# One encoder layer on one core: the preparations for the last MLP chunks by turns, and the residual added at a chunk's end

## The chip, the core and the metric

The program runs on one core of a Trainium2 chip. The metric is the device time of one execution in microseconds; the figure given for a kernel is the median of its runs.

The engines are TensorE (PE; its weight loads are PEld), VectorE (DVE), ScalarE (ACT), GpSimd (POOL) and SyncE (SP), which issues every DMA here. Each engine works through its own queue in the order of the program, so an instruction that waits holds up all that stands behind it on that engine.

## The reference, cut to what matters

Two request groups, 512 and 1024 tokens of width 1024, go through one layer with shared weights. The time in question lies in the MLP and what directly follows it:

```python
h = h + concat([o_attn, o_pool]) @ w_out
m = rmsnorm(h, norm_mlp_g)
h = h + square(relu(m @ w_up)) @ w_down          # D_FF = 4096
gate = sigmoid(rmsnorm(h, norm_ple_g) @ w_ple_gate)
h = h + gate * (p @ w_ple_proj)                  # then the final rmsnorm
```

All operands are float32.

## The kernel before, in words

**Precision.** TensorE gets fp32r operands. A float32 operand is split into a high part (an ACT cast) and a low part (operand minus high part, on DVE or POOL), and a product is three matmuls: high·high, high·low, low·high.

**Layout.** The 1536 tokens are three chunks (c = 0, 1, 2) of 512 tokens, kept transposed with 128 features on the partitions. Data lives in 49 equal slots of SBUF that tiles take and give back; a new tile waits until the slot's last user, a DMA too, is done.

**The MLP.** It follows the attention stage. A `Pair` (c, g) is two of the 32 blocks of 128 hidden features of one chunk; 16 pairs make a chunk, pair number n runs from 0 to 47. The up product of a pair is done by Strassen-Winograd: seven products `i` in the order `UP = (1, 6, 2, 5, 7, 3, 4)`, each 12 matmuls of 128x256, with operands `w` (weights) and `mo` (inputs, stored by `make_m`). DVE takes the sums out of PSUM (tiles `u`, `c`). Product 3 goes on top of the PSUM bank of product 5 and product 4 on top of that of product 7, so TensorE can start them only after DVE has read those banks (the additions into `u` and into `c[:, B]` after products 5 and 7).

In chunk 0 the down product is plain. In chunks 1 and 2 two pairs together form a `Double`, whose down product is also Winograd: seven products in the order `DOWN = (1, 5, 2, 3, 7, 6, 4)`, 24 matmuls each (tile `pd`), with weights `v` and inputs `ta`. Up and down products alternate on TensorE: the fourteen up products of a double are steps k = 0 to 13, and after each odd k one down product of the double before is issued.

Two streams prepare the operands, one piece at each `next`:

- `weights()` loads four quarters `we` of w_down, forms their sums on DVE (tiles `vs`, `we`) and splits each into `v`: per half an ACT cast and a POOL subtraction.
- `inputs()` splits the activations `c` into `ta`: an ACT cast, a DVE subtraction, and DVE differences.

Both are called once after every step (`after(i)`), so a `v` takes two steps and a `ta` with its difference takes two steps. The streams of a double begin at its own k = 10 and 11, so that two `v` and two `ta` lie ready ahead of its first down product.

**The residual.** mean(h²)+eps is a row `w` of one value per token. The MLP is computed on unnormalised h, so the result has to be divided by `w`. Before, the accumulators start as h·w (`raise_h` for chunk 0; `load_quarters` and `raise_to` for chunks 1 and 2, which store the accumulators as five tiles `H..`: 22, 11, 12, 21 and u), every down product is added to them on DVE, `invert` replaces `w` by its reciprocal, and in the end the accumulator is multiplied by it (`finishing`, `finishing_from`, `stat_h`).

**Chores.** Work that is not urgent is a queue of generators, `chores`; `step()` runs one piece of the first of them after each product. In chunk 1 these are `finishing(0)` and `make_m(2)`, in chunk 2 `finishing_from(1)`.

**DMA.** The split up-weights of pairs 1 to 15 are kept in DRAM by chunk 0 (`kept_d`) and fetched again by chunks 1 and 2: seven loads of 512 KB for each pair, some pieces ahead.

## Time and profile before

| | |
|---|---|
| median of 3 runs | 1802.34 us (1800.7 to 1809.57) |
| profiled execution | 1805.42 us, its span 1803.5 us |
| mean granted TensorE clock | 0.991 |
| PE / DVE / ACT / POOL busy | 96% / 75% / 50% / 59% of the span |
| DMA | 390.73 MB, 217 GB/s on average |
| chunk 0 of the MLP | about 580 to 917 us |
| chunks 1 and 2 | about 917 to 1580 us |
| gate stage and end | from about 1580 us |

A busy PE is not yet a PE at its peak, because matmuls are pipelined. In chunks 1 and 2 all matmuls have one form, 128x256, so their number in a stretch of equal length is the better measure: 338 or 339 in 40 us where nothing is in the way. The prediction counts them.

### The profile page before, as it was taken

The page shows a single profiled execution, that of the slowest core. Times are in us where ns is not written, and L with a number is a line of the kernel's source. Part 1 is how long each engine was busy: PE and PEld are TensorE (multiplying, and loading weights), DVE is VectorE, ACT ScalarE, POOL GpSimd, SP SyncE. Part 2 cuts the span into 40 slices and gives each one's busy share as a digit, 9 for nine tenths or more (in the row PEclk, how much of TensorE's full clock was granted, in tenths as well). Part 3 has the DMA queues.
Part 4 walks back from the last instruction along what each step waited for, and adds up shares of the span by engine and source line. Part 5 has one row for each costly group of instructions (what it writes and reads, how often), then busy time and mean ns, then how long its engine had stood idle before and what let it go on. Part 6 is the DMA issues. An engine that isn't in the chain of part 4 may idle for free. (4 is left out here: it accounts for less than half of the span.)

```text
span 1803.5 us, 31527 instructions
## 1 busy us (share of the span) xinstructions
PE 1736.2 (96%) x11692; PEld 1577.2 (87%) x11692; DVE 1356.7 (75%) x1880; ACT 910.3 (50%) x1830; POOL 1055.1 (59%) x907
## 2 busy tenths in 40 slices
PE   9999999999999899999998999999999999999997
PEld 6888777888868788988998999999999999987797
DVE  5667765888895876876548887889988877876755
ACT  6343455768794455655435454545444444433232
POOL 3474873535675757775626668867577555652421
PEclk9999999999999999999999999999999999999998
DMA  6232645120418899897799877799767777643102
GB/s 249 100 125 105 221 163 191 43 95 13 175 66 329 317 307 340 317 343 270 279 388 328 299 245 255 267 314 362 269 234 273 242 256 238 232 150 111 59 9 86
DMA packets 133608, 390.73 MB, mean 217 GB/s; under 512 B 14160, under 2 KB 26832, under 8 KB 133456
## 3 DMA queue, kind: packets, MB, share of 16 engines
q1 hardware_dynamic: 133456, 388.73, 60.7%
q8 instruction: 92, 1.51, 0.3%
q14 instruction: 60, 0.49, 0.1%
HBM read 274.38 MB, written 114.29 MB: 216 GB/s over the span
## 5 line engine op out<-in xcount | busy, mean ns | idle before, releaser
L49 PE MATMUL pd<-ta,v 128*128 128x256 f32 x2688 | 341.9, 283 | 4.1 <-DVE ta L1023 3.7
L49 PEld LDWEIGHTS pd<-ta,v 128*128 128x128 f32 x2688 | 331.2, 191 | 5.7 <-DVE ta L1023 4.6
L1008 POOL TENSOR_TENSOR v<-we,v 128x512 fp32r<-128x512 f32 x128 | 198.3, 1559 | 88.6 <-ACT v L1007 79.7
L1008 POOL TENSOR_TENSOR v<-vs,v 128x512 fp32r<-128x512 f32 x96 | 141.7, 1480 | 148.9 <-ACT v L1007 137.9
L1023 DVE TENSOR_TENSOR ta<-c,ta 128x512 fp32r<-128x512 f32 x112 | 143.3, 1280 | 73.6 <-ACT ta L1022 70.6
L49 PE MATMUL pd<-r,wd 128*128 128x512 f32 x768 | 191.2, 396 | 4.6 <-DVE r L916 4.1
L461 POOL TENSOR_SCALAR pr<-pr,rr 128x512 f32<-128x512 f32 x160 | 111.5, 708 | 134.1 <-DVE rr L456 64.4
L49 PE MATMUL z<-w,x 128*128 128x512 f32 (+1 forms) x864 | 175.8, 359 | 1.9 <-ACT w L159 1.4
L49 PE MATMUL pq<-mo,w 128*128 128x256 f32 x1152 | 157.0, 287 | 16.7 <-DVE c L951 14.7
L49 PEld LDWEIGHTS pd<-r,wd 128*128 128x128 f32 x768 | 139.6, 188 | 35.8 <-DVE r L916 6.4
L49 PEld LDWEIGHTS z<-w,x 128*128 128x128 f32 x864 | 143.2, 189 | 28.8 <-ACT w L159 3.5
L49 PEld LDWEIGHTS pq<-mo,w 128*128 128x128 f32 x1152 | 146.7, 193 | 18.6 <-DVE c L951 16.1
L49 PE MATMUL pz<-mo,w 128*128 128x256 f32 x1152 | 153.4, 282 | 3.5 <-DVE u L946 3.2
L49 PE MATMUL px<-mo,w 128*128 128x256 f32 x1152 | 152.8, 282 | 1.3 <-DMA w<-kept_d 1.3
L49 PEld LDWEIGHTS pz<-mo,w 128*128 128x128 f32 x1152 | 145.2, 189 | 8.8 <-DVE u L946 5.4
L815 POOL TENSOR_TENSOR w<-ws,w 128x512 fp32r<-128x512 f32 x72 | 102.2, 1423 | 79.9 <-ACT w L814 66.4
L49 PEld LDWEIGHTS px<-mo,w 128*128 128x128 f32 x1152 | 144.7, 189 | 3.2 <-issue 1.4
L49 PE MATMUL pg<-hg,wg 128*128 128x512 f32 (+1 forms) x768 | 142.0, 340 | 0.0
L49 PEld LDWEIGHTS pg<-hg,wg 128*128 128x128 f32 x768 | 119.8, 190 | 17.0 <-DVE s L1525 0.3
L472 ACT CAST pt<-tp 128x512 fp32r<-128x512 f32 x160 | 88.0, 591 | 88.5 <-PE tp L53 86.7
L473 DVE TENSOR_TENSOR pt<-tp,pt 128x512 fp32r<-128x512 f32 x160 | 104.1, 684 | 31.3 <-ACT pt L472 31.0
L441 DVE TENSOR_REDUCE nm<-S 128x1 f32<-128x1024 f32 (+1 forms) x96 | 100.0, 1042 | 23.3 <-PE S L49 22.7
(234 smaller groups left out, 3573.5 us busy)
## 6 DMA issues: line engine op xcount, KB each, us to landing
w<-kept_d SPq DMA_DIRECT2D x210, 512.0 KB, 5.1
kept_d<-w SPq DMA_DIRECT2D x105, 512.0 KB, 5.0
we<-in_w_down_dram SPq DMA_DIRECT2D x64, 512.0 KB, 5.4
mo_d<-mm SPq DMA_DIRECT2D x84, 256.0 KB, 4.8
mo<-mo_d SPq DMA_DIRECT2D x42, 512.0 KB, 8.7
wur<-in_w_up_dram SPq DMA_DIRECT2D x36, 512.0 KB, 5.9
wdr<-in_w_down_dram SPq DMA_DIRECT2D x32, 512.0 KB, 7.2
h_d<-h SPq DMA_DIRECT2D x16, 512.0 KB, 2.9
```

What stands on the lines that cost most here:

```text
L49: last_pe[0] = nc.tensor.matmul(*a, **k).ins
L441: ve.tensor_reduce(nm, S[:, :nch * CH], axis=AX.X, op=ALU.max, negate=True)
L461: gp.tensor_scalar(p, p, rr, 1.0, op0=ALU.mult, op1=ALU.mult)
L472: sc.copy(self.pt[kt][:, 0], tp)
L473: ve.tensor_tensor(self.pt[kt][:, 1], tp, as32(self.pt[kt][:, 0]), op=ALU.subtract)
L815: gp.tensor_tensor(t[:, 1], x, as32(t[:, 0]), op=ALU.subtract)
L1008: gp.tensor_tensor(t[:, 1], src[:, p], as32(t[:, 0]), op=ALU.subtract)
L1023: ve.tensor_tensor(t[:, 1], x, as32(t[:, 0]), op=ALU.subtract)
```

## The change

- **Accumulators.** The first down product of a chunk that goes to an accumulator is copied to it by ACT; `raise_h`, `load_quarters` and `raise_to` are gone, and with them the loads of h at each chunk's start. The residual comes back when a chunk is finished: `finishing(0)` and `lower_from` (chunk 1) multiply by 1/w and then add h, reloaded as `rest`, on POOL. For chunk 2 a new chore `raise_late` multiplies the reloaded h by w on DVE and adds it on POOL, after `finishing_from(1)`.
- **Reciprocals.** They move from `invert` into `make_m`.
- **Turns.** At odd k both streams are called twice, at even k not at all. An ACT cast and a sum take a whole `v` (128x1024) in one instruction; the low part stays two POOL instructions of 128x512, and the first of them waits for the newest DVE instruction of `inputs()`. The streams of a double begin at k = 11, and the loads `we` come up to one step earlier.
- **Layout of `v`.** High and low parts are two tiles of their own instead of halves of two tiles.

```diff
+    wr_d = dram.tile([P, CH], F32, name="wr_d")
...
         ve.tensor_scalar(acc[:, 1], bc, 1.0 / D, EPS, op0=ALU.mult, op1=ALU.add)
+        if c == 2:
+            sy.dma_start(wr_d, acc[:, 1])
+        for b in range(4):
+            yield
+            w = acc[:, 1, b * P:(b + 1) * P]
+            ve.reciprocal(w, w)
         sy.dma_start(w_d[c], acc[:, 1])
...
-    def raise_h(c, e=ve):
-        for a in range(4):
-            for h in range(2):
-                e.tensor_tensor(hT[c][a][:, h], hT[c][a][:, h], ws[c], op=ALU.mult)
-                yield
...
-    def load_quarters(c):
-        HS[c] = {nm: slot([P, D], F32, f"H{c}{nm}") for nm in ("22", "11", "12", "21")}
-        for (q, x), t in HS[c].items():
-            for a in range(2):
-                load(quarters(t[:, a * CH:(a + 1) * CH]), h_d[c][2 * (int(q) - 1) + a][:, :, TOK[x]])
-        HS[c]["u"] = slot([P, D], F32, f"H{c}u")
...
-    def raise_to(c):
-        for nm in ("22", "11", "12", "21"):
-            for a in range(2):
-                scaled(c, nm, a)
-                yield
...
     def lower_from(c, nm, e):
         H = HS[c]
+        r = rest(c, nm) if c < 2 else None
         for a in range(2):
+            part = slice(a * CH, (a + 1) * CH)
+            t = H[nm][:, part]
             if nm != "11":
-                t = H[nm][:, a * CH:(a + 1) * CH]
-                e.tensor_tensor(t, t, H["u"][:, a * CH:(a + 1) * CH], op=ALU.add)
+                e.tensor_tensor(t, t, H["u"][:, part], op=ALU.add)
                 yield
             scaled(c, nm, a)
             yield
+            if r is not None:
+                e.tensor_tensor(t, t, r[:, part], op=ALU.add)
+                yield
+    def rest(c, nm):
+        r = slot([P, D], F32, f"rest{c}{nm}")
+        for a in range(2):
+            load(quarters(r[:, a * CH:(a + 1) * CH]), h_d[c][2 * (int(nm[0]) - 1) + a][:, :, TOK[nm[1]]])
+        return r
+    def raise_late(c):
+        w = slot([P, CH], F32, f"wr{c}")
+        load(w, wr_d)
+        for nm in ("22", "11", "12", "21"):
+            r = rest(c, nm)
+            yield from wait(4)
+            for a in range(2):
+                part = slice(a * CH, (a + 1) * CH)
+                t = quarters(r[:, part])
+                ve.tensor_tensor(t, t, w[:, TOK[nm[1]]].unsqueeze(1).to_broadcast([P, 2, HF]), op=ALU.mult)
+                yield
+                gp.tensor_tensor(HS[c][nm][:, part], HS[c][nm][:, part], r[:, part], op=ALU.add)
+                yield
...
-    def invert(c):
-        for b in range(4):
-            w = ws[c][:, b * P:(b + 1) * P]
-            ve.reciprocal(w, w)
-            yield
-        sy.dma_start(w_d[c], ws[c])
...
-            h = hT[self.c][a]
-            ve.tensor_tensor(h, pd.rearrange("p (a b) -> p a b", a=2), h, op=ALU.add)
+            pd = pd.rearrange("p (a b) -> p a b", a=2)
+            if self.g == 0:
+                h = hT.setdefault(0, {})[a] = slot([P, 2, CH], F32, f"h0{a}m")
+                sc.copy(h, pd)
+            else:
+                h = hT[0][a]
+                ve.tensor_tensor(h, pd, h, op=ALU.add)
...
-            def total(i, p):
-                e = SUMS[i]
-                if i == 1:
-                    e.tensor_tensor(s[0][:, p], e21[:, p], e22[:, p], op=ALU.add)
-                elif i == 2:
-                    e.tensor_tensor(s[1][:, p], s[0][:, p], e11[:, p], op=ALU.subtract)
-                elif i == 4:
-                    e.tensor_tensor(s[0][:, p], e12[:, p], s[1][:, p], op=ALU.subtract)
-                else:
-                    e.tensor_tensor(e21[:, p], e11[:, p], e21[:, p], op=ALU.subtract)
-            at = 0
             for i in DOWN:
                 if i == 5:
                     s.append(slot([P, 2, CH], F32, f"vs{self.id}1"))
+                total = {1: (s[0], e21, e22, ALU.add), 5: (s[-1], s[0], e11, ALU.subtract),
+                         2: (s[0], e12, s[-1], ALU.subtract), 3: (e21, e11, e21, ALU.subtract)}
                 src = {1: e11, 5: s[0], 2: e12, 3: s[0], 7: e21, 6: s[-1], 4: e22}[i]
-                self.v[i] = []
+                hi, lo = self.v[i] = [slot([P, 2, CH], F32R, f"v{self.id}_{i}{k}") for k in range(2)]
+                sc.copy(hi, src)
+                if i in total and i != 2:
+                    out, x, y, op = total[i]
+                    ve.tensor_tensor(out, x, y, op=op)
+                yield
                 for p in range(2):
-                    t = slot([P, 2, CH], F32R, f"v{self.id}_{i}{p}")
-                    self.v[i].append(t)
-                    sc.copy(t[:, 0], src[:, p])
-                    gp.tensor_tensor(t[:, 1], src[:, p], as32(t[:, 0]), op=ALU.subtract)
-                    for what in AT.get(at, ()):
-                        total(*what)
-                    at += 1
-                    yield
+                    ins = gp.tensor_tensor(lo[:, p], src[:, p], as32(hi[:, p]), op=ALU.subtract).ins
+                    if p == 0 and last_ve[0] is not None:
+                        tc.add_manual_dep(ins, last_ve[0].name, SYNC, reason="port")
+                if i == 2:
+                    out, x, y, op = total[i]
+                    ve.tensor_tensor(out, x, y, op=op)
+                yield
...
-            diffs = {1: (b11, b12, b11), 3: (b12, b22, b12), 7: (b11, b22, b11), 6: (b21, b21, b11)}
+            diffs = {3: (b12, b22, b12), 7: (b11, b22, b11), 6: (b21, b21, b11)}
             for i, x in ((1, b11), (5, b11), (2, b21), (3, b22), (7, b12), (6, b11), (4, b21)):
+                if i == 5:
+                    ve.tensor_tensor(b11, b12, b11, op=ALU.subtract)
                 t = self.t7[i] = slot([P, 2, 2, HF], F32R, f"ta{self.id}_{i}")
                 sc.copy(t[:, 0], x)
-                ve.tensor_tensor(t[:, 1], x, as32(t[:, 0]), op=ALU.subtract)
                 yield
+                last_ve[0] = ve.tensor_tensor(t[:, 1], x, as32(t[:, 0]), op=ALU.subtract).ins
                 if i in diffs:
                     out, y, z = diffs[i]
-                    ve.tensor_tensor(out, y, z, op=ALU.subtract)
+                    last_ve[0] = ve.tensor_tensor(out, y, z, op=ALU.subtract).ins
                 yield
...
-                    ws_ = [w[p][:, k, j * P:(j + 1) * P] for k in range(2)]
+                    ws_ = [w[k][:, p, j * P:(j + 1) * P] for k in range(2)]
...
-                h = HS[self.c][{1: "u", 6: "u", 2: "11", 5: "22", 7: "22", 3: "12", 4: "21"}[i]]
-                if i == 1 and self.m == 0:
-                    sc.copy(h, pd)
+                to = {1: "u", 6: "u", 2: "11", 5: "22", 7: "22", 3: "12", 4: "21"}[i]
+                H = HS.setdefault(self.c, {})
+                if to not in H:
+                    H[to] = slot([P, D], F32, f"H{self.c}{to}")
+                    sc.copy(H[to], pd)
                 else:
+                    h = H[to]
                     ve.tensor_tensor(h, pd, h, op=ALU.add)
...
-    SUMS = {1: ve, 2: ve, 3: ve, 4: ve}
-    AT = {0: ((1, 0),), 1: ((1, 1),), 2: ((2, 0),), 3: ((2, 1),), 4: ((4, 0),), 5: ((4, 1),), 6: ((3, 0),), 7: ((3, 1),)}
...
-    LEADS, STEPS = (4, 3), (1, 1)
+    STEPS, last_ve = (1, 1), [None]
+    SYNC = mybir.DependencyInfo(mybir.DependencyClass.Sync, mybir.DependencyReason.DATA)
...
-    LOADS = {3: (0, 0), 6: (0, 1), 8: (1, 1), 10: (1, 0)}
+    LOADS = {3: (0, 0), 5: (0, 1), 7: (1, 1), 9: (1, 0)}
...
+            r = slot([P, 2, CH], F32, f"rest{c}{a}")
+            load(r, h_d[c][a])
             for e in range(2):
                 ve.tensor_tensor(h[:, e], h[:, e], ws[c], op=ALU.mult)
+                yield
+                gp.tensor_tensor(h[:, e], h[:, e], r[:, e], op=ALU.add)
                 yield
...
-        if c == 0 and g == 0:
-            load_ms(c)
-            late_h = raise_h(c)
-        if g == 1:
-            if c:
-                load_ms(c)
-                load_quarters(c)
-                raising = raise_to(c)
-            else:
-                chores.append(invert(c))
...
-        if g == 3 and c:
-            chores.append(invert(c))
...
+            chores.append(raise_late(2))
...
-            if n == 0:
-                load_h(0, i, h_d[0][i])
-            if n == 1:
-                next(late_h)
-                next(late_h)
...
-            if raising and UP.index(i) % 2:
-                next(raising, None)
...
-                if last_db or k >= 14 - LEADS[0]:
+                feed_w, feed_x = k % 2 and (last_db or k >= 11), k % 2 and (last_db or k >= 11)
+                if feed_x:
+                    next(inputs)
+                if feed_w:
                     next(weights)
-                if last_db or k >= 15 - LEADS[1]:
+                if feed_x:
                     next(inputs)
+                if feed_w:
+                    next(weights)
...
-        for _ in range(2):
-            next(weights, None)
-            next(inputs, None)
+        for stream in (inputs, weights, inputs, weights):
+            next(stream, None)
```

Three places show what moves. The first is DVE's queue in the second pair of chunk 2 (`u2_1`, `c2_..` are that pair's tiles, the `vs2_0.` sums of the next double's weights, `H222` an accumulator); before:

```order
L946 TENSOR_TENSOR u2_1_14566<-pz2_1_14682,u2_1_14566 128x256
L658 TENSOR_TENSOR H222_14553<-H222_14553,w2_14551 128x512
L990 TENSOR_TENSOR vs2_00_14702<-we2_001_14543,we2_011_14629 128x512
L1023 TENSOR_TENSOR ta1_7_4_14707<-c1_71_13773,ta1_7_4_14707 128x512
L951 TENSOR_TENSOR c2_01_14314<-pq2_1_14710,u2_1_14566 128x256
```

The same place now:

```order
L1029 TENSOR_TENSOR ta1_7_4_14538<-c1_71_13685,ta1_7_4_14538 128x512
L1060 TENSOR_TENSOR H122_10731<-pd1_77_14546,H122_10731 128x1024
L956 TENSOR_TENSOR u2_1_14451<-pz2_1_14571,u2_1_14451 128x256
L961 TENSOR_TENSOR c2_01_14224<-pq2_1_14588,u2_1_14451 128x256
L1006 TENSOR_TENSOR vs2_00_14606<-we2_001_14398,we2_011_14468 128x1024
L1029 TENSOR_TENSOR ta2_0_1_14604<-c2_00_14223,ta2_0_1_14604 128x512
```

Three SBUF instructions stood between the two readings of PSUM (`u` and `c`, products 5 and 7); now none does, and the sum, twice as wide, stands behind them.

The second is SP's queue early in chunk 1, about the second pair; before:

```order
L56 DMA we1_001_10403<-in_w_down_dram 128x2x512
L56 DMA w1_10419<-w_d1_260 128x512
L56 DMA H122_10421<-h_d1_2_310 128x2x256
L56 DMA H122_10421<-h_d1_3_311 128x2x256
L56 DMA H111_10422<-h_d1_0_308 128x2x256
L56 DMA H111_10422<-h_d1_1_309 128x2x256
L56 DMA H112_10423<-h_d1_0_308 128x2x256
L56 DMA H112_10423<-h_d1_1_309 128x2x256
L56 DMA H121_10424<-h_d1_2_310 128x2x256
L56 DMA H121_10424<-h_d1_3_311 128x2x256
L56 DMA w0_10434<-w_d0_259 128x512
L56 DMA w1_1_7_10451<-kept_d1_7_320 128x1024
```

Now (`rest00` is the residual for `finishing(0)`):

```order
L56 DMA w1_1_5_10393<-kept_d1_5_320 128x1024
L56 DMA w0_10409<-w_d0_260 128x512
L56 DMA w1_1_7_10426<-kept_d1_7_321 128x1024
L56 DMA we1_011_10428<-in_w_down_dram 128x2x512
L56 DMA rest00_10431<-h_d0_0_305 128x1024
L56 DMA w1_1_3_10448<-kept_d1_3_322 128x1024
```

Eight loads ahead of the up-weights `w1_1_7` are gone; one of 512 KB comes in behind it.

The third is POOL's queue at the start of the first double of chunk 1; before:

```order
L1008 TENSOR_TENSOR v1_0_20_10618<-we1_010_10514,v1_0_20_10618 128x512
L1008 TENSOR_TENSOR v1_0_21_10649<-we1_010_10514,v1_0_21_10649 128x512
L1352 TENSOR_TENSOR sqg0_10453<-sqg0_10453,sqg01_10626 128x512
L1008 TENSOR_TENSOR v1_0_30_10696<-vs1_00_10516,v1_0_30_10696 128x512
L1352 TENSOR_TENSOR sqg0_10453<-sqg0_10453,sqg01_10626 128x512
L1008 TENSOR_TENSOR v1_0_31_10723<-vs1_00_10516,v1_0_31_10723 128x512
```

Now:

```order
L1009 TENSOR_TENSOR v1_0_21_10613<-we1_010_10467,v1_0_20_10612 128x512 x2
L1354 TENSOR_TENSOR h01m_6915<-h01m_6915,rest01_10591 128x512
L1009 TENSOR_TENSOR v1_0_31_10685<-vs1_00_10505,v1_0_30_10684 128x512 x2
L1354 TENSOR_TENSOR h01m_6915<-h01m_6915,rest01_10591 128x512
L1009 TENSOR_TENSOR v1_0_71_10765<-we1_001_10376,v1_0_70_10764 128x512 x2
```

The low parts of a `v` now come in twos, and additions of the reloaded residual, each waiting for a DMA, stand between them.

More of the change, by code (lines that the diff above doesn't have):

```diff
@@ L1399, in encoder_layer @@
     START, MORE = 1, (2, 2)
-    before, pending, raising = None, deque(), None
+    before, pending = None, deque()
     for n, pair in enumerate(pairs):
         c, g = pair.c, pair.g
-        if c == 0 and g == 0:
-            load_ms(c)
-            late_h = raise_h(c)
-        if g == 1:
-            if c:
-                load_ms(c)
-                load_quarters(c)
-                raising = raise_to(c)
-            else:
-                chores.append(invert(c))
         if (c, g) == (1, 1):
@@ L1483, in encoder_layer @@
             pass
-        if g == 3:
-            for _ in raising or ():
-                pass
-            raising = None
         before = pair
```

## The prediction

> **What bounds the kernel now.** I read the head of the page first: who is busy.
>
> ```profile
> span 1803.5 us, 31527 instructions
> PE 1736.2 (96%) x11692; PEld 1577.2 (87%) x11692; DVE 1356.7 (75%) x1880; ACT 910.3 (50%) x1830; POOL 1055.1 (59%) x907
> ```
>
> TensorE is the bound: whatever the other engines save counts only where TensorE stands still or runs slowly for their sake. So the next view is the table of stretches over chunks 1 and 2 (start:end, length, PE busy and number of matmuls, then PEld, DVE, ACT, POOL, granted clock, DMA share, GB/s).
>
> ```profile
> 960.00:1000.00 40.00, 33.59 (x260) 32.37 (x259) 36.40 (x40) 17.78 (x34) 25.23 (x16) 0.93 0.85 309
> 1080.00:1120.00 40.00, 39.27 (x329) 39.03 (x328) 30.46 (x32) 20.78 (x41) 34.14 (x24) 1.00 0.69 230
> 1120.00:1160.00 40.00, 37.08 (x301) 36.88 (x300) 32.02 (x34) 21.07 (x41) 29.55 (x21) 0.96 0.86 314
> 1160.00:1200.00 40.00, 38.45 (x321) 38.04 (x320) 33.21 (x35) 21.18 (x42) 34.79 (x24) 1.00 0.88 288
> 1320.00:1360.00 40.00, 36.97 (x295) 36.36 (x295) 36.82 (x41) 17.58 (x32) 28.73 (x21) 0.96 0.73 253
> 1360.00:1400.00 40.00, 38.40 (x324) 38.19 (x323) 35.37 (x38) 16.71 (x33) 28.94 (x22) 1.00 0.69 249
> 1440.00:1480.00 40.00, 40.00 (x339) 40.00 (x338) 30.62 (x37) 17.32 (x35) 21.74 (x15) 1.00 0.72 238
> ```
>
> The last row is the undisturbed state: 339 matmuls of 128x256 in 40 us, 0.118 us each. Against it 79 are missing from 960 to 1000 (9.3 us), 10 + 38 + 18 = 66 from 1080 to 1200 (7.8 us), 44 + 15 = 59 from 1320 to 1400 (7.0 us): 24 us in all. This count holds both the idle time and the slow matmuls behind it, for the granted clock is 0.93 and 0.96 in three of these rows and 1.00 in the undisturbed one. These 24 us, and little else, are what a better order of the preparations can win.
>
> The waits of TensorE between 955 and 1560 us say for whom (total, times, longest):
>
> ```profile
> PE pq L49 <- DVE c L951: 12.8, 5, 4.1
> PE pz L49 <- DVE u L946: 3.2, 7, 1.0
> ```
>
> Both are DVE reading a PSUM bank on which TensorE wants to accumulate the next up product. DVE's own timeline shows why it is late, ahead of the longest of them and of the one in chunk 2:
>
> ```profile
> 990.77 1.56 DVE L658 TENSOR_TENSOR H<-H,w 128x512 f32<-128x512 f32 x1
> 992.25 1.75 DVE L990 TENSOR_TENSOR vs<-we,we 128x512 f32<-128x512 f32 x1
> 993.92 1.74 DVE L1023 TENSOR_TENSOR ta<-c,ta 128x512 fp32r<-128x512 f32 x1
> 995.59 0.74 DVE L1327 SCALAR_TENSOR_TENSOR hg<-h,gple_sb,hg 128x512 fp32r<-128x512 f32 x1
> 996.26 0.41 DVE L951 TENSOR_TENSOR c<-pq,u 128x256 f32<-128x256 f32 x1
> ...
> 1328.69 1.58 DVE L658 TENSOR_TENSOR H<-H,w 128x512 f32<-128x512 f32 x1
> 1330.19 1.75 DVE L990 TENSOR_TENSOR vs<-we,we 128x512 f32<-128x512 f32 x1
> 1331.86 0.68 DVE L1023 TENSOR_TENSOR ta<-c,ta 128x512 fp32r<-128x512 f32 x1
> 1332.46 0.41 DVE L951 TENSOR_TENSOR c<-pq,u 128x256 f32<-128x256 f32 x1
> ```
>
> Preparations (raising the accumulator, a weight sum, an input's low part) stand in the queue ahead of the urgent reading, and most of them take 1.6 to 1.75 us.
>
> **The change part by part.** Prices first (minimum/median/maximum in ns):
>
> ```profile
> L658 DVE TENSOR_TENSOR H<-H,w x32: 674/693/1786, 943.8 to 1708.9; 128x512 f32<-128x512 f32 x32
> L1052 DVE TENSOR_TENSOR H<-pd,H x80: 1154/1211/1226, 971.0 to 1653.8; 128x1024 f32<-128x1024 f32 x80
> L1050 ACT COPY H1u<-pd x1: 1008/1008/1008, 961.9 to 961.9; 128x1024 f32<-128x1024 f32 x1
> L1023 DVE TENSOR_TENSOR ta<-c,ta x112: 672/1365/1861, 953.9 to 1635.5; 128x512 fp32r<-128x512 f32 x112
> L1008 POOL TENSOR_TENSOR v<-we,v x128: 1262/1730/1826, 948.1 to 1628.3; 128x512 fp32r<-128x512 f32 x128
> ```
>
> A DVE instruction with two SBUF operands has two prices, 0.67 and about 1.75, and so has POOL's, 1.26 and 1.73; the one that reads PSUM has a single price, 1.15 to 1.23. So DVE and POOL slow each other down in SBUF, and the urgent readings of PSUM suffer only from what stands ahead of them.
>
> *Start of chunk 1, loads.* The eight loads of H sit in SP's queue ahead of the up-weights, and TensorE then waits for those weights:
>
> ```profile
> 927.69 9.03 SPq L56 DMA_DIRECT2D H<-h_d  x8
> 937.73 1.06 SPq L56 DMA_DIRECT2D w<-kept_d  x2
> 951.49 1.67 PE L49 MATMUL px<-mo,w 128*128 128x256 f32 x12 [1.26 <-DMA w<-kept_d]
> 954.49 1.70 PE L49 MATMUL py<-mo,w 128*128 128x256 f32 x12 [1.33 <-DMA w<-kept_d]
> ```
>
> The 9.0 us of issuing become one load of 512 KB. The two waits, 2.6 us, can at most vanish; the weights come up to 9 us earlier, so I take 2.5.
>
> *Start of chunk 1, DVE (960 to 1000).* DVE loses the eight raisings of chunk 1 (0.67 to 1.56 us each here, so between 5.4 and 12.5 us) and four first additions, 4 x 1.21 = 4.8 us, which become copies on ACT at 1.01 us, an engine that is busy for 17.8 of the 40 us. That is 10 to 17 us off an engine that was busy for 36.4 of 40 and late by 4.1 at the worst place. Bounds: 0 and 9.3; I take 7.5, near the upper end, since the relief is more than twice the longest lateness, less a part for the first two `v`, which now begin a step later.
>
> *Chunk 1, 1080 to 1200.* There is nothing to raise here. The worst wait is one for a slot:
>
> ```profile
> 1122.31 1.45 DVE L990 TENSOR_TENSOR vs<-we,we 128x512 f32<-128x512 f32 x1 [3.76 <-DMA mo_d<-mm]
> 1124.76 2.93 PE L49 MATMUL pq<-mo,w 128*128 128x256 f32 x12 [2.92 <-DVE c L951]
> ```
>
> The sum needed a slot that a store had not yet freed, and the reading of `pq` stood behind it. In the new order no sum stands between the two readings in the second pair of a double; the sum comes after, where the next urgent reading has a down product (24 x 0.118 = 2.8 us) and two up products (1.4 each) before TensorE needs it; these 5.7 us I call a round. In the first pair the feeding at k = 3 does stand between them, but with a down product in between: product 7, down and product 3 give the same 5.7 us or more. The feeding then is a sum of 128x1024 (two of 128x512: 1.35 to 3.5 us) and two of 128x512 (1.35 to 3.5): 2.7 us if POOL is quiet, 7.0 if it is not. So slot waits of up to 3 us are hidden when POOL is quiet and partly show when it is not. Bounds 0 and 7.8; I take 5.
>
> *Chunk 2, 1320 to 1400.* The raisings go (they become `raise_late`, a chore in the later, undisturbed part), and the order is the new one. Bounds 0 and 7.0; I take 5.
>
> *Chunk 0.* The eight raisings and the four loads of its first pairs go, and ACT makes four copies. The longest wait of TensorE among the second pair's down products, where the raisings run, is this:
>
> ```profile
> 620.94 2.13 PE L49 MATMUL pd<-r,wd 128*128 128x512 f32 x8 [0.89 <-DVE r L916]
> ```
>
> Its releaser belongs to the chain of the activation, not to the raising; bounds 0 and 0.9, and I count nothing.
>
> *The rest of chunk 2 and the gate stage.* Undisturbed rows stay so; the gate stage keeps its instructions. Nothing. The reciprocals only change their place, as chores of DVE: nothing, as long as DVE is not late there.
>
> Sum of the gains: 2.5 + 7.5 + 5 + 5 = 20 us.
>
> *What is added.* POOL gets 8 additions for each chunk, 24 x 1.26 to 1.73 = 30 to 42 us. Their cover is POOL's own waiting (in the stretch from 940 to 1600 us):
>
> ```profile
> POOL v L1008 <- ACT v L1007: 208.6, 80, 21.1
> ```
>
> With 208.6 us of it I cost them at nothing; without that cover they cost up to 42. The waits that come with them are another matter. `finishing(0)` loads each of its four `rest` one step before POOL wants it, and `lower_from` does so for the part "11"; a like load takes 5.9 us to land:
>
> ```profile
> m<-h_d SPq DMA_DIRECT2D x12, 512.0 KB, 5.9
> ```
>
> A step is 2.9 us with its share of the down products, so POOL may stand for 3 us, five times, and behind it the next `v`. A `v` is begun two rounds ahead, 2 x 5.7 = 11.4 us; its sum, its two partners on DVE and its two POOL halves take 2.7 + 2.5 = 5.2 us without contention and 7.0 + 3.5 = 10.5 with it. So the standing is hidden or shows in part: 0 to 15 us, and I take 2, since both cases have to coincide. The new wait of POOL for DVE holds up the chores behind it, and DVE in turn waits for POOL before a sum may overwrite a source (product 2's) and at each multiplication in `lower_from`. The trace of before has no such ring; its bounds are nothing and, for 16 doubles with one such sum each of up to 1.7 us late, 27. I take 0, for the readings behind it have 5.7 us.
>
> Net: 20 - 2 = 18 us. Made against the profiled execution (1805.42 us, span 1803.5) that is 1787; this execution was 3.1 us above the median of the runs, 1802.34, so the forecast for the median is 1784 us.
>
> A rule speaks against the turns. The Trainium skill, "SBUF — State Buffer", section "SBUF: two separate sides", says that the port pair shared by VectorE and GpSimd is an exclusive lock held for the whole instruction and not a division of the bandwidth. The two prices above agree in that there is a quick and a slow one. They don't in full: 0.67 us of DVE inside 1.26 us of POOL would make 1.93 for the one that waits and 1.26 for the other, and the rows have 1.73 to 1.78 for both. By that rule turns win nothing in total, and the first rival below is what it would do here.
>
> **The rivals.** *Slower: POOL becomes the bound in the parts with chores.* From 1160 to 1200 POOL is already busy for 34.8 of 40 us. In a round of 5.7 us it has two halves of a `v` and two chores, 4 x 1.26 = 5.0 us if DVE keeps off and 4 x 1.73 = 6.9 if not, and now it waits for DVE as well. It decides as soon as a round takes longer than 5.7 us for so many rounds that the 11.4 us ahead are used up; then the added 30 to 42 us reach TensorE and the gains are lost in part: 30 - 20 = 10 to 42 - 20 = 22 us slower, about 1816. Against it: a stretch of chores in which every piece has POOL work is short, the long ones were survived before at the same load, and 208.6 us of waiting are free.
>
> *No change that counts: the lateness only moves.* The wide sum (1.35 to 3.5 us) and the slot waits stay, now in front of other readings. Then only the loads (2.5 us) and half of 960 to 1000 (4.6) are won, less 2: about 1797. For it speaks that the worst wait from 1080 to 1200 is a DMA's.
>
> *All of it.* 2.5 + 9.3 + 7.8 + 7.0 = 27 us: about 1775.
>
> **How the numbers follow.** I give the forecast 0.53, all of it 0.13, the mere move 0.21, the slower case 0.13. A measurement of this kernel can tell about 0.5%, 9 us, from no change: faster is under 1793, slower over 1811. Faster gets 0.53 + 0.13 = 0.66, the same 0.21, slower 0.13. The range reaches from 1768 (all of it, and some of the waits outside the three stretches) to 1804, which takes in the mere move with the full 7 us of its uncertainty; the slower case stays outside.
>
> **What would show it.** In the profile after, 960 to 1000 should have over 320 matmuls and 1320 to 1360 over 330; TensorE's waits for the reading of `pq` (now L961) should fall from 12.8 us to under 4; the `w<-kept_d` waits at the start of chunk 1 should be gone; and these two means should fall, the first towards 0.9 us and the second towards 1.35:
>
> ```profile
> L1023 DVE TENSOR_TENSOR ta<-c,ta 128x512 fp32r<-128x512 f32 x112 | 143.3, 1280 | 73.6 <-ACT ta L1022 70.6
> L1008 POOL TENSOR_TENSOR v<-we,v 128x512 fp32r<-128x512 f32 x128 | 198.3, 1559 | 88.6 <-ACT v L1007 79.7
> ```
>
> POOL should show some 3 us of waiting for each `rest`. I am wrong if TensorE waits for `pd` with POOL's `v` as the releaser, or if the undisturbed rows of 339 fall.

## The result and the profile after

| | median | runs | ratio to before, 95% interval |
|---|---|---|---|
| before | 1803.8 us | 7, 1800.7 to 1809.57 | |
| changed | 1792.95 us | 7, 1791.55 to 1798.7 | 0.9939, 0.9922 to 0.9957 |

The change makes the kernel about 11 us faster. The forecast was 1784 (18 us faster), its range 1768 to 1804. The profiled execution of the changed kernel took 1798.7 us (span 1796.9, mean granted clock 0.990). It is the longest of the seven, so its rows show a little more trouble than the median has.

The head of the page:

```profile
span 1796.9 us, 31417 instructions
PE 1735.9 (97%) x11692; PEld 1579.1 (88%) x11692; DVE 1261.6 (70%) x1788; ACT 908.7 (51%) x1730; POOL 1063.9 (59%) x931
```

VectorE lost 95 us of work, and the time moved by 11. Where the rest went is seen in the stretches over chunks 1 and 2 (same columns as in the prediction):

```profile
920.00:960.00 40.00, 40.00 (x305) 38.47 (x305) 25.34 (x30) 17.95 (x30) 15.35 (x11) 1.00 1.02 384
960.00:1000.00 40.00, 36.72 (x294) 36.31 (x294) 27.06 (x31) 22.13 (x35) 28.76 (x20) 0.96 0.76 285
1000.00:1040.00 40.00, 37.84 (x304) 37.53 (x304) 30.57 (x35) 16.44 (x27) 25.09 (x17) 0.96 0.81 289
1040.00:1080.00 40.00, 37.95 (x306) 37.52 (x305) 26.09 (x34) 16.12 (x28) 22.32 (x18) 0.96 0.77 275
1080.00:1120.00 40.00, 40.00 (x338) 40.00 (x338) 26.37 (x33) 22.90 (x40) 29.50 (x23) 1.00 0.62 211
1120.00:1160.00 40.00, 39.78 (x334) 39.57 (x334) 29.95 (x31) 19.80 (x35) 29.63 (x22) 1.00 0.96 346
1160.00:1200.00 40.00, 38.89 (x325) 38.48 (x324) 30.61 (x32) 22.82 (x39) 34.66 (x24) 1.00 0.73 249
1200.00:1240.00 40.00, 37.81 (x315) 37.31 (x313) 30.53 (x35) 18.51 (x33) 27.15 (x20) 1.00 0.98 369
1240.00:1280.00 40.00, 38.57 (x318) 37.90 (x319) 32.75 (x36) 18.48 (x32) 29.86 (x20) 1.00 0.87 327
1320.00:1360.00 40.00, 37.34 (x312) 36.94 (x311) 28.92 (x32) 14.82 (x24) 32.00 (x24) 1.00 0.65 229
1360.00:1400.00 40.00, 36.85 (x293) 36.23 (x292) 27.53 (x31) 18.20 (x30) 28.82 (x22) 0.96 0.75 264
```

The rows of before that the prediction doesn't show:

```profile
920.00:960.00 40.00, 35.98 (x257) 33.41 (x256) 21.95 (x32) 14.16 (x27) 9.94 (x8) 1.00 1.04 382
1000.00:1040.00 40.00, 40.00 (x333) 40.00 (x332) 31.35 (x38) 19.19 (x37) 26.58 (x19) 0.98 0.85 293
1040.00:1080.00 40.00, 39.90 (x333) 39.61 (x333) 34.86 (x39) 22.68 (x44) 26.47 (x19) 1.00 0.75 244
1200.00:1240.00 40.00, 39.69 (x332) 39.40 (x331) 33.75 (x43) 18.17 (x37) 22.01 (x15) 1.00 0.87 332
1240.00:1280.00 40.00, 39.75 (x334) 39.55 (x334) 36.65 (x40) 20.55 (x41) 32.28 (x21) 1.00 0.91 326
```

Won, in matmuls against before: 305 for 257 from 920 to 960, 294 for 260 from 960 to 1000, 334 for 301 from 1120 to 1160. Lost: 304 and 306 for 333 and 333 from 1000 to 1080, 315 and 318 for 332 and 334 from 1200 to 1280, and 293 for 324 from 1360 to 1400. The first and the last loss are where `finishing(0)` and `finishing_from(1)` run; the one between them is around the start of chunk 2, and the experiments will show that it has another origin. TensorE's waits from 920 to 1600 us name a new releaser, ScalarE:

```profile
PE px L49 <- ACT u L941: 9.4, 8, 2.9
PE pz L49 <- DVE u L956: 4.9, 3, 2.2
PE pq L49 <- DVE c L961: 2.9, 4, 2.0
PE pd L49 <- POOL v L1009: 1.9, 2, 1.1
```

The longest of the new waits, followed back through three queues. TensorE, ScalarE and GpSimd around 966 us:

```profile
973.50 2.00 PE L49 MATMUL px<-mo,w 128*128 128x256 f32 x12 [2.94 <-ACT u L941]
```

```profile
966.59 1.06 ACT L1358 ACTIVATE sqg<-h01m 128x1024 f32<-128x1024 f32 x1 [7.80 <-POOL h01m L1354]
967.55 1.32 ACT L1332 ACTIVATE hg<-h01m,gple_sb 128x512 fp32r<-128x512 f32 x2
...
970.99 1.00 ACT L1057 COPY H<-pd 128x1024 f32<-128x1024 f32 x1
...
973.10 0.35 ACT L941 COPY u<-px 128x256 f32<-128x256 f32 x1
```

```profile
962.77 2.54 POOL L1009 TENSOR_TENSOR v<-vs,v 128x512 fp32r<-128x512 f32 x2 [1.38 <-DVE c L1032]
965.26 1.29 POOL L1354 TENSOR_TENSOR h01m<-h01m,rest 128x512 f32<-128x512 f32 x1
```

Read from below. GpSimd's second residual addition (L1354) stands behind the two halves of a `v`, which wait by the new order for VectorE. ScalarE's square of the sum (L1358) waits for that addition for 7.8 us, and with it the whole queue: two scalings for the gate, a relu and a square of `c`, the casts of `ta` and `v`, the new first copy of `H`, another relu and square. Only then comes the copy of `px` (L941), for which TensorE has been standing. The same happens at 1022 us, where ScalarE waits 5.25 us for `h03m`. There the late cast of `ta` keeps VectorE waiting 6.21 us, and behind that stands the reading of `pz` (a stall of 2.15 us at 1028.14).

In chunk 2 it is VectorE that waits, in `lower_from`, for GpSimd's addition of `u`: 12.7 us in six times.

A stall costs more than its length. In stretches of 10 us around these two the granted clock (third column from the end) falls:

```profile
960.00:970.00 10.00, 10.00 (x86) 10.00 (x86) 3.20 (x5) 3.38 (x6) 5.18 (x4) 1.00 0.58 209
970.00:980.00 10.00, 7.06 (x47) 6.86 (x46) 7.63 (x9) 8.06 (x14) 8.28 (x6) 0.83 0.98 370
...
1020.00:1030.00 10.00, 7.84 (x64) 7.64 (x63) 3.97 (x5) 5.89 (x9) 5.43 (x5) 0.96 0.68 217
1030.00:1040.00 10.00, 10.00 (x76) 10.00 (x76) 9.86 (x11) 3.59 (x7) 6.30 (x4) 0.87 0.72 263
```

From 1030 to 1040 TensorE is never idle and still makes 76 matmuls for the 86 of an undisturbed row. From 960 to 1080 there are 904 matmuls for 3 x 339 = 1017: 113 x 0.118 = 13.3 us lost, with 7.5 us of idle time over 0.3 us each.

### The profile page after: what moved, and what is told of

It is laid out like the page before. It is cut to its first block, busy times and chain, and to the rows that moved or that the text cites. A ratio compares the mean times of both kernels' runs of the same rounds, so it can differ in the third digit from the quotient of the medians.

```text
span 1796.9 us, 31417 instructions
## 1 busy us (share of the span) xinstructions
PE 1735.9 (97%) x11692; PEld 1579.1 (88%) x11692; DVE 1261.6 (70%) x1788; ACT 908.7 (51%) x1730; POOL 1063.9 (59%) x931
## 5 line engine op out<-in xcount | busy, mean ns | idle before, releaser
L1009 POOL TENSOR_TENSOR v<-we,v 128x512 fp32r<-128x512 f32 x128 | 185.0, 1467 | 103.4 <-DVE ta L1029 26.0
L1009 POOL TENSOR_TENSOR v<-vs,v 128x512 fp32r<-128x512 f32 x96 | 128.7, 1363 | 111.5 <-DVE c L1032 37.2
L1029 DVE TENSOR_TENSOR ta<-c,ta 128x512 fp32r<-128x512 f32 x112 | 108.1, 965 | 88.4 <-ACT ta L1027 82.1
```

Source lines behind the costliest of these rows:

```text
L1009: ins = gp.tensor_tensor(lo[:, p], src[:, p], as32(hi[:, p]), op=ALU.subtract).ins
L1029: last_ve[0] = ve.tensor_tensor(t[:, 1], x, as32(t[:, 0]), op=ALU.subtract).ins
```

## The experiments

The theory after this: the additions of the residual cost little as work, but each is a hop to another engine between two instructions of engines whose queues carry urgent readings. Rivals: the work itself costs, wherever it is done; GpSimd is overloaded; the turns' own wide sums make the stalls; only the accumulators bring the gain. Of each kernel 4 to 12 runs were compared with runs of the kernel before on the same chip.

| kernel | median us | ratio to before, 95% interval |
|---|---|---|
| copies_only / copies_added | 1815.12 / 1812.07 | 1.0057 (1.0043 to 1.007) / 1.0044 (1.0029 to 1.0059) |
| turns_only / turns_raised | 1789.69 / 1791.17 | 0.9912 (0.9896 to 0.9928) / 0.9923 (0.9905 to 0.9941) |
| norest | 1774.16 | 0.9831 (0.9811 to 0.9852) |
| sq_later | 1789.36 | 0.9906 (0.9885 to 0.9927) |
| lower | 1790.71 | 0.9914 (0.9897 to 0.9931) |
| add_dve | 1783.47 | 0.9877 (0.9859 to 0.9894) |
| untangled | 1782.17 | 0.988 (0.9858 to 0.9901) |
| dve_later | 1781.08 | 0.9861 (0.9841 to 0.988) |
| mixed_noport | 1788.12 | 0.99 (0.9881 to 0.9919) |
| **mixed** | **1776.32** | **0.9834 (0.9817 to 0.9851)** |

### Either half alone

The streams `weights()` and `inputs()`, their calls, the layout of `v` and the `LOADS` come from one kernel, all the rest from the other. The lines that tell them apart, as taken over or left:

```diff
-                if last_db or k >= 14 - LEADS[0]:
-                    next(weights)
-                if last_db or k >= 15 - LEADS[1]:
-                    next(inputs)
+                feed_w, feed_x = k % 2 and (last_db or k >= 11), k % 2 and (last_db or k >= 11)
+                if feed_x:
+                    next(inputs)
+                if feed_w:
+                    next(weights)
...
+                    if p == 0 and last_ve[0] is not None:
+                        tc.add_manual_dep(ins, last_ve[0].name, SYNC, reason="port")
```

> Only the accumulators: first products copied, residual added at a chunk's end, reciprocals moved; both preparation streams, their calls at every step and the layout of v as before. Theory (queue blocking: the new GpSimd additions sit between a VectorE and a ScalarE instruction and so hold up urgent copies): the wins at the start of chunk 1 appear, the losses from 1000 to 1080 too, the stall near 1122 stays: about 1799 us, 4 less than before. Rival A (the gain is the accumulators' alone, the turns do nothing): 1793, as the changed kernel. Rival B (the accumulators cost more than they bring): 1804 or more.

> Only the turns: both streams twice at odd k, whole-tile casts and sums, the wait of v for the newest VectorE instruction, the new layout; accumulators raised and loaded as before. Theory: 1080 to 1160 gains its 5 us as in the changed kernel, 960 to 1000 stays as bad as before, no new stalls behind the copy of px: about 1798. Rival A (turns do nothing): 1803. Rival C (the wide sums and the wait of v themselves make the new stalls): 1805 or more, with stalls for px and pz as in the changed kernel.

In this first pair a few lines of chunk 0's down product were exchanged too: copies_only adds chunk 0's first products to a tile with stale contents, and turns_only copies them and so lacks chunk 0's residual. The second pair has these lines in their place:

> The turns alone on the kernel before, with its accumulators in all three chunks (turns_only also had chunk 0's copies, and so lacked chunk 0's residual; chunk 0 took 2.6 us less there). Theory 1 (the turns bring the gain, the accumulators cost): 1790 to 1793. Rival A (the turns_only time came from what it lacked): 1800 or more.

> The accumulators alone as in copies_only, but with chunk 0's first products copied too, which copies_only had left as additions to an accumulator with stale contents. Theory 1 (with the preparations in the old order the later additions make VectorE and ScalarE late just as in the changed kernel): 1810 to 1817, slower than before. Rival A (the 1815 came from that slip): 1805 or less.

The turns alone make 1791.17 us, by the ratio some 14 less than before: theory 1 holds, rival A falls. In the first pair I had expected 1798 and no gain from 960 to 1000, and both were wrong: turns_only takes 1789.69 and has 313 matmuls there for 260 before (turns_raised 309). The turns have a loss of their own too: turns_raised has 276 matmuls for 321 from 1160 to 1200, with stalls of 1.93 us for the reading of `pz` and 3.30 us for that of `pq`; the changed kernel has 325 there. The accumulators alone are 7 to 10 us slower than before, as rival B of copies_only had it. I had expected 4 faster in the first pair, and this was wrong; the stale tile was not the reason. In copies_added TensorE waits four times as long for the reading of `pz` as before (3.2 us), and about as long for that of `pq`:

```profile
PE pz L49 <- DVE u L956: 12.4, 10, 3.8
PE pq L49 <- DVE c L961: 11.7, 6, 4.3
```

The longest, 4.34 us at 1206.73, has a sum in front that waits 3.59 us for a load of `we`; in another, at 1401.57, a multiplication of `lower_from` and two slowed preparations stand there. How much of the 7 to 10 us goes to each I have not separated. By place, the largest loss is from 1200 to 1280, around the start of chunk 2: 268 + 309 = 577 matmuls for 666 before, 89 x 0.118 = 10.5 us. The changed kernel has 633 there and turns_raised 678, so this loss comes with the new accumulators, the moved reciprocals included. So the turns account for the whole gain, and the accumulators, as they are written, for none of it.

### Without the additions

```diff
-                gp.tensor_tensor(h[:, e], h[:, e], r[:, e], op=ALU.add)
...
-                e.tensor_tensor(t, t, r[:, part], op=ALU.add)
```

> The changed kernel without the 16 GpSimd additions of the residual in chunks 0 and 1 (finishing(0) and lower_from leave them out, the loads of rest stay; the output lacks that residual; chunk 2 keeps its eight). Theory (queue blocking by these additions): the waits of TensorE for the copy of px fall from 9.4 to under 5 us, the rows from 1000 to 1080 rise from 305 to over 325 matmuls, 1360 to 1400 from 293 to over 320: about 1783 us, 10 less than the changed kernel. Rival C (the turns' own wide sums): within 3 us of the changed kernel's 1793.

1774.16 us, 19 less than the changed kernel; the theory had said 10, rival C at most 3. TensorE's waits for the copy of `px` fall to 3.1 us, and where the finishing chores run the rows are whole:

```profile
960.00:1000.00 40.00, 40.00 (x338) 40.00 (x338) 30.83 (x37) 24.09 (x38) 28.65 (x19) 1.00 0.92 350
1000.00:1040.00 40.00, 40.00 (x339) 40.00 (x338) 32.31 (x40) 19.51 (x32) 25.05 (x17) 1.00 0.91 327
...
1320.00:1360.00 40.00, 40.00 (x339) 40.00 (x338) 28.36 (x35) 18.43 (x31) 27.29 (x22) 1.00 0.83 286
1360.00:1400.00 40.00, 40.00 (x339) 40.00 (x338) 28.08 (x37) 16.89 (x28) 24.85 (x22) 1.00 0.70 261
```

These 16 additions, some 16 x 1.3 to 2.3 us of GpSimd's time, cost 19 us of the kernel's. The loss from 1200 to 1280 is not theirs: without them there are 312 + 319 = 631 matmuls, as in the changed kernel. This alone doesn't tell work from hop; the next four do.

### The hop or the work

The later square: the store, square and first gate input of part a come after the additions of part a + 1.

```diff
-            sy.dma_start(hl_d[c][a], h)
-            sq = slot([P, 2, CH], F32, f"sqg{c}{a}") if a else acc
-            sc.activation(sq, h, AF.Square)
...
+            if a:
+                yield from tail(a - 1)
+        yield from wait(2)
+        yield from tail(3)
```

> The changed kernel with one edit: in finishing(0) the square, the first gate input and the store of a part come after the next part's additions, with the same additions. Theory (ScalarE's square stands waiting for GpSimd's addition, and the copy of px behind it): ScalarE's waits of 7.8 and 5.3 us ahead of the square vanish, and with them the stalls of TensorE at 973 and 1028 (2.9 and 2.2 us) and the slow matmuls behind: 960 to 1080 gains 30 matmuls or more, about 1788. Rival D (GpSimd is overloaded there, whatever waits for it): the stalls move to pd behind v, 1792 or more.

```profile
960.00:1000.00 40.00, 40.00 (x339) 40.00 (x338) 34.04 (x38) 22.69 (x36) 31.79 (x20) 1.00 0.91 346
1000.00:1040.00 40.00, 40.00 (x337) 39.95 (x337) 34.47 (x40) 20.44 (x33) 30.08 (x22) 1.00 0.92 331
1040.00:1080.00 40.00, 40.00 (x337) 39.91 (x336) 24.87 (x35) 18.96 (x32) 20.38 (x18) 1.00 0.69 238
```

From 960 to 1080 there are 339 + 337 + 337 = 1013 matmuls for 904 (theory: at least 30 more), and the stalls at 973 and 1028 are gone, with GpSimd doing the same additions: rival D falls for this place. A part comes back as a loss: from 1120 to 1240 this kernel and the three later ones with the later square have 947 to 952 matmuls, where the changed kernel has 974 and norest 975, some 3 us; why is not shown. The median, 1789.36, is 3.6 us lower, but the two intervals overlap, and its profiled execution (1781.4) is the quickest of its six; the time alone would not have shown it.

The order in `lower_from` (before, the three operations of a half followed each other; `add` is GpSimd's addition of one half):

```diff
...
+        for a in range(2) if nm != "11" else ():
+            add(a, H["u"])
+            yield
+        for a in range(2):
+            scaled(c, nm, a)
+            yield
+        for a in range(2):
+            add(a, r)
+            yield
```

> The changed kernel with one edit: in lower_from the two additions of u, the two multiplications and the two residual additions of a part are issued in that order, so that each finds its operand two steps old. Theory 1: VectorE's waits for GpSimd's H shrink from 12.7 us to under 2, 1320 to 1400 goes from 605 matmuls towards the 678 without the additions: 6 us less than the changed kernel, 1787. Rival D (GpSimd overloaded): 1793, the stalls stay.

VectorE's waits of 12.7 us for GpSimd's `H` are gone. But 1320 to 1400 has 640 matmuls, not 678, and 1790.71 us is not told apart from the changed kernel. The wait went one engine on, to ScalarE's square of the part, which now stands behind the last addition (the changed kernel had 8.5 us there):

```profile
ACT sqh L703 <- POOL H L660: 12.1, 4, 4.4
```

The same additions on VectorE:

```diff
-                gp.tensor_tensor(h[:, e], h[:, e], r[:, e], op=ALU.add)
+                ve.tensor_tensor(h[:, e], h[:, e], r[:, e], op=ALU.add)
...
-                e.tensor_tensor(t, t, r[:, part], op=ALU.add)
+                ve.tensor_tensor(t, t, r[:, part], op=ALU.add)
```

> The changed kernel with the 16 residual additions of chunks 0 and 1 on VectorE, right behind its multiplication, instead of on GpSimd; order and steps unchanged. Theory 1 (the change of engine costs: who needs the sum waits for GpSimd's queue, and the urgent copies behind it): nearly all of the 19 us that leaving them out won, less 16 x 0.7 to 1.7 us more on VectorE of which a part shows: 1776 to 1784. Rival E (the work itself costs, wherever it is done): 1790 or more. Rival D (GpSimd is overloaded): like theory 1, but the waits of v on GpSimd's queue shrink too.

1783.47 us, 9.5 less, though VectorE is the engine that TensorE waits for: moving the same work back to VectorE, which takes out the hop, gave back about half of the 19 us, and rival E, which wanted 1790, falls. GpSimd stood idle ahead of the `v` from `we` for 103.4 us in the changed kernel already (121.8 here), so on the whole it was not overloaded. In chunk 2 the rows are nearly whole, from 960 to 1000 they are not:

```profile
960.00:1000.00 40.00, 37.38 (x312) 36.97 (x312) 27.83 (x37) 22.20 (x35) 24.50 (x17) 1.00 0.78 286
1320.00:1360.00 40.00, 40.00 (x337) 39.92 (x336) 29.96 (x36) 18.93 (x30) 28.01 (x20) 1.00 0.79 267
1360.00:1400.00 40.00, 39.19 (x330) 38.99 (x329) 30.87 (x37) 18.01 (x30) 26.48 (x21) 1.00 0.79 275
```

> The changed kernel with three edits: the later square in finishing(0), the order in lower_from, and the reciprocals written beside their source instead of over it (VectorE stood 2.2 us for the store of that source). All additions stay on GpSimd. Theory 1: 1776 to 1781, within 6 us of the kernel without the additions (1774). Rival D: 1786 or more.

1782.17 us lies between the theory's 1781 and rival D's 1786. From 960 to 1080 it has 1008 matmuls, from 1320 to 1400 only 627, for `lower` is in it. Its third edit, after which VectorE's stand of 2.21 us ahead of a reciprocal and TensorE's stall of 1.6 us at 1229 are no longer seen:

```diff
-            w = acc[:, 1, b * P:(b + 1) * P]
-            ve.reciprocal(w, w)
-        sy.dma_start(w_d[c], acc[:, 1])
+            p = slice(b * P, (b + 1) * P)
+            ve.reciprocal(acc[:, 0, p], acc[:, 1, p])
+        sy.dma_start(w_d[c], acc[:, 0])
```

### The better half of each

`mixed` is sq_later with the reciprocals beside their source and the second of add_dve's two edits, the one in `lower_from`; `dve_later` has its first edit too. The edit of the reciprocals was never run alone, so its share is not known.

> The better half of each: in finishing(0) the later square with the additions on GpSimd, in lower_from the additions on VectorE, and the reciprocals written beside their source. Theory 1 (each addition is cheap once nobody urgent waits behind it): 960 to 1080 keeps the 1013 matmuls of sq_later, 1320 to 1400 the 667 of add_dve against 605 in the changed kernel: 1775 to 1780, near the 1774 without the additions. Rival E (the work itself costs): 1783 or more, no better than either half.

> The same with the additions of finishing(0) on VectorE too. Theory 1: ScalarE no longer waits for the sum, but VectorE has 8 more instructions ahead of its urgent readings from 960 to 1080, so a part of the 59 matmuls that add_dve lacked there against sq_later stays away: 1776 to 1784, not faster than the mixed kernel. Rival F (only the place of the square counts, not the engine): equal to it within 2 us.

`mixed` leaves nothing out and takes 1776.32 us, 29 us or 1.7% less than before, 15 less than the turns alone, and some 2 us above the kernel that leaves the 16 additions out (by the ratios the same). Its rows where the changed kernel had 294, 304 and 306:

```profile
960.00:1000.00 40.00, 39.59 (x333) 39.52 (x333) 34.73 (x39) 23.78 (x36) 29.78 (x20) 1.00 0.95 353
1000.00:1040.00 40.00, 40.00 (x337) 39.84 (x337) 35.74 (x38) 20.33 (x33) 30.84 (x21) 1.00 0.89 319
1040.00:1080.00 40.00, 40.00 (x337) 39.91 (x336) 24.87 (x35) 18.34 (x31) 20.45 (x17) 1.00 0.71 246
```

In these three rows VectorE is busy for 95.3 us (83.7 in the changed kernel) and GpSimd for 81.1 (76.2): the same additions, now with nobody urgent behind them. From 1320 to 1400 it has 338 + 332 = 670 for 605. So the theory holds. VectorE's wait for GpSimd's addition of `u` is still there (9.2 us; norest 7.5, turns_raised 10.5), so the wait by itself costs little: what counts is what stands behind it. From 1200 to 1280 the kernel has 320 + 324 = 644 matmuls, for 678 with the turns alone; the stalls there are for `v` now. `dve_later` is not faster (1781.08); its rows from 960 to 1080 sum to 1005 for mixed's 1007 and the intervals overlap, so whether the engine of these eight additions still matters stays open.

### The wait alone

```diff
-                    ins = gp.tensor_tensor(lo[:, p], src[:, p], as32(hi[:, p]), op=ALU.subtract).ins
-                    if p == 0 and last_ve[0] is not None:
-                        tc.add_manual_dep(ins, last_ve[0].name, SYNC, reason="port")
+                    gp.tensor_tensor(lo[:, p], src[:, p], as32(hi[:, p]), op=ALU.subtract)
```

> The mixed kernel without the wait of v's first half for the newest VectorE instruction of the inputs; the order stays. Theory 1 (the turns win by their order and by the shorter operations alike): VectorE's low part of ta goes back from 0.95 to 1.1 us or more and 1 to 5 us of the time are lost. Rival G (the order alone brings the turns' gain): within 1 us. Rival H (the wait costs, since GpSimd stands for it 60 to 130 us): 2 us or more faster.

12 us are lost, not 1 to 5: theory 1 was right in the sign and too small, G and H fall. The groups of the mixed kernel, then of the one without the wait:

```profile
L1009 POOL TENSOR_TENSOR v<-we,v 128x512 fp32r<-128x512 f32 x128 | 184.4, 1463 | 97.5 <-DVE ta L1029 26.4 <-DVE c L1032 24.8 <-DMA w<-kept_d 9.8
L1029 DVE TENSOR_TENSOR ta<-c,ta 128x512 fp32r<-128x512 f32 x112 | 108.5, 969 | 72.8 <-ACT ta L1027 71.4
L1032 DVE TENSOR_TENSOR c<-c,c 128x512 f32<-128x512 f32 x48 | 38.2, 796 | 0.0
```

```profile
L1009 POOL TENSOR_TENSOR v<-we,v 128x512 fp32r<-128x512 f32 x128 | 200.9, 1592 | 83.3 <-ACT v L1003 60.0 <-issue 22.2 <-DMA wpr<-in_w_proj_dram 0.4
L1027 DVE TENSOR_TENSOR ta<-c,ta 128x512 fp32r<-128x512 f32 x112 | 128.5, 1147 | 68.6 <-ACT ta L1025 66.5 <-issue 0.7
L1030 DVE TENSOR_TENSOR c<-c,c 128x512 f32<-128x512 f32 x48 | 56.3, 1173 | 0.0
```

With the wait GpSimd stands for VectorE (26.4 and 24.8 us) and VectorE's `ta` and differences take 0.97 and 0.80 us; without it they take 1.15 and 1.17, and TensorE's wait for the reading of `pq` grows from 1.9 to 9.8 us. So the wait, which by itself only delays GpSimd, is worth 12 us here, where the turns as a whole brought 14 on the kernel before.

## Why the prediction was right or wrong, point by point

The direction, the range and the cause (VectorE's preparations ahead of urgent readings) were right. The 18 us came out as 11 because two sums were too small, and they partly cancelled: without the 16 additions the gain is 31 us where I had 20, and the additions cost 19 us where I had 2. That the result is as near to the forecast as it is, is thus in part luck.

- **Start of chunk 1, loads: 2.5 us, bounds 0 to 2.6.** Too small. The waits for `w<-kept_d` went as said. From 920 to 960 the changed kernel has 48 more matmuls, of which the 1.9 us earlier end of chunk 0 explains only a part (the row still holds chunk 0's last 128x512 matmuls, so its counts are rough): norest, whose chunk 0 ends as late as before, has 299, or 42 x 0.118 = 5.0 us more; turns_raised, which keeps the loads, has 263.
- **Start of chunk 1, VectorE: 7.5 us, bounds 0 to 9.3.** As a term right (norest has 338 matmuls for 260, 9.2 us), in the kernel not reached: 294, where I named over 320. It isn't the accumulators' alone either: turns_raised, which raises, has 309.
- **Chunk 1, 1080 to 1200: 5 us.** Right: 338 + 334 + 325 for 951 matmuls before, 46 x 0.118 = 5.4 us.
- **Chunk 2, 1320 to 1400: 5 us.** Not in the kernel: 605 for 619 before, and 312 from 1320 to 1360 where I named over 330. Without the additions 678, the full 7 us.
- **The reciprocals: nothing, as long as VectorE is not late there.** It was late there. From 1200 to 1280 the changed kernel has 33 matmuls fewer than before (3.9 us), and its longest stall in these rows, 1.60 us at 1229, follows the reciprocal that stood 2.21 us for the store of its own source. In untangled and mixed, which write it elsewhere, neither is seen. The other stalls there take 0.18 to 0.87 us each; their cause is open.
- **Chunk 0: nothing.** From its first up product to its last down product it took 2.5 us less (352.5 for 355.0). I had bounded it by 0.9.
- **What is added: 2 us. This is the step that failed.** The additions' own time was indeed hidden, as the row of GpSimd's waiting said, and the `rest` loads made GpSimd stand once, 13.6 us before the first, and not five times 3. The waits were the cost, 19 us by norest: the ring, which I had taken as 0 with bounds to 27, and one that I had not listed. I named VectorE's wait in `lower_from` and gave it nothing, since "the readings behind it have 5.7 us"; and I never listed what stands behind ScalarE's square in its queue. A list of ScalarE's queue from L1358 on would have shown the copy of `px` as the tenth instruction behind it. I also priced a stall by its length, though I had counted the slow matmuls behind it among the gains.
- **The slower rival** didn't occur, and the undisturbed rows stay at 338 to 340. TensorE's waits for `pd` with `v` as releaser, which I had named as a sign of being wrong, did appear, but with 1.9 us in two times (none before) they are no bound. The 10 to 22 us that I gave this rival make 1812 to 1824, with 1818 and not 1816 in the middle. **The lateness only moves** (1797) is nearer in time than the forecast, but not by its mechanism: the lateness of the sums did go, another came.
- **The signs.** The wait for `pq` fell to 2.9 us (under 4 as said); the mean of `ta` is 0.965 us (towards 0.9), that of `v` 1.467 (towards 1.35, not quite half of the way).
- **The exclusive lock.** By the Trainium skill, "SBUF — State Buffer", section "SBUF: two separate sides", read as I read it, the turns win nothing in total. I had doubted the rule because both engines have a slow price. That was a misreading, as a stretch of before shows in which both are never idle:

```profile
967.10 1.75 POOL L1352 TENSOR_TENSOR sqg<-sqg,sqg 128x512 f32<-128x512 f32 x1
967.62 1.78 DVE L996 TENSOR_TENSOR we<-we,we 128x512 f32<-128x512 f32 x1
968.80 1.75 POOL L1008 TENSOR_TENSOR v<-vs,v 128x512 fp32r<-128x512 f32 x1
969.32 1.78 DVE L1327 SCALAR_TENSOR_TENSOR hg<-h,gple_sb,hg 128x512 fp32r<-128x512 f32 x1
```

They end by turns, at 968.85, 969.40, 970.55 and 971.10: VectorE's 0.55 us after GpSimd's, GpSimd's 1.15 us after VectorE's, one for one, 1.70 us the pair. This is how it would look if only one worked at a time and each in turn waited for the other, and it makes both slow; so these rows agree with the page. mixed_noport measures 12 us for the wait. The page isn't refuted by that, since the total was the wrong question: what counts is which of the two engines stands, and GpSimd has the time for it.

## What to carry to other kernels

Before an operation moves to an idle engine, list what stands in the queue behind the instruction that will read its result: the cost of the move is that queue's lateness rather than the operation's time. Here most of it went away in one place by issuing the reader one piece later, and in the other by leaving the operation on the engine of the one before it. Where two engines slow each other down, let the one with time to spare wait for the other. When two halves of a change can be run apart, run them: here the turns alone won 14 us, the accumulators alone lost 7 to 10, and only with the additions and the reciprocals placed better did both together win 29.

## What was unexpected of the hardware

In the changed kernel the stretches of 10 us that hold or follow stalls of 2.94 and 2.15 us show a granted clock of 0.83 and 0.87, and from 960 to 1080 7.5 us of idle time cost 13.3. In norest and the mixed kernel, whose longest stalls from 920 to 1560 are 1.64 and 1.33 us, all rows of 40 us show 1.00. The length alone doesn't decide it: sq_later shows 0.86 in the stretch of a stall of 1.96 us at 1336 and 1.00 in that of one of 2.21 us at 1376.
